# Projections of the differential attention written between the steps of the gated attention's block loop

## The chip, the cores and the metric

The kernel runs on one core of one Trainium2 chip. The metric is the time of one execution on the device in microseconds (us); less is better. Three executions of the kernel before took 1509.5, 1514.04 and 1517.23 us, the median is 1514.04 us. One more execution was recorded by the profiler.

The engines have short names in the profile: PE is TensorE (matrix products), PEld its weight loads, DVE is VectorE, ACT is ScalarE, POOL is GpSimd, SP is the engine whose queue issues most DMA transfers.

## What is computed

Two layers of an encoder on 512 positions of width 1024. Each layer has a mixer and a squared-ReLU MLP, each between norms. The mixer projects the normed input `h` once and splits the result among four head groups; their outputs are joined and projected back.

```
proj = h @ w_in
(a_q, a_k, a_v, a_qi, a_ki, a_wi, b_q, b_k, b_v, b_g,
 c_q, c_k, c_v, c_a, c_g, d_q, d_k, d_v) = jnp.split(proj, ...)
y_a = head_norm(dsa_mixer(a_q, a_k, a_v, a_qi, a_ki, a_wi, pos))     # sparse attention, top-128 selection
y_b = silu(b_g) * head_norm(retention_mixer(b_q, b_k, b_v, pos))
y_c = silu(c_g) * head_norm(gla_mixer(c_q, c_k, c_v, c_a, ...))      # gated linear attention
y_d = head_norm(diff_mixer(d_q, d_k, d_v, pos, ...)) * (1 - lam_init) # differential attention
y = jnp.concatenate([y_a, y_b, y_c, y_d], axis=-1) @ w_out
```

The change touches two of them. The gated linear attention (C) has, within chunks of 64 positions, scores whose decay depends on both positions, and carries a state from chunk to chunk. The differential attention (D) turns its queries and keys by a rotary step (rope), takes two softmax maps per head, subtracts one from the other with a learned factor, and applies the result to its values.

## The kernel before, in words

Everything is in fp32, but the large products are made of three matmuls on split operands: each operand is a high part (a cast on ScalarE) and a low part (the rest, subtracted on VectorE or GpSimd), and `mm3` (line 267) adds high x high, high x low and low x high in PSUM.

`mixers` (line 572) writes the mixer of a layer. The input projection is cut into column groups. A group of 256 columns is projected by `proj_tm` (line 536): for each of four blocks of 128 positions, 24 matmuls (8 slices of the depth, three each) into one of two PSUM buffers of the pool `pj`, and then an eviction that the caller gives. Groups 4, 5 and 6 are the queries, keys and values of D, group 10 the values of C, group 2 the queries of A. The weights of a group come in four tiles, by `prep` (line 254): a DMA of 256 KB on SP's queue into `raw`, the cast to `whi` on ScalarE (line 262), the subtraction to `wlo` on VectorE or GpSimd (line 264). `whi` and `wlo` have a ring of six buffers each, so a group's last tiles can be written only when the group before has been multiplied. `ahead` (line 682) writes the preparation of the next group in a fixed order (10, 4, 5, 6, 2, ...), and `PLAN["lo"]` says on which engine the low parts are made: for group 4 the first on VectorE and three on GpSimd, for group 5 the third on VectorE, for 6 and 2 all on GpSimd. `run` (line 695) is `ahead` and then a projection of all four blocks.

The gated attention is a loop over four blocks `b` (line 901), and in each over four score steps `c` (line 905). `decay` (line 877) makes a block's decay factors: matmuls `fs`, exponentials into `F` on ScalarE, then products into `KF` and `q4` (in the profile `q`) on GpSimd and VectorE; `decay(0)` and the projection of group 10 stand ahead of the loop. A score step copies four pieces of the queries into one of three `QF` tiles on ScalarE (line 913), multiplies them with `KF` into a PSUM tile `sg` (lines 918 and 922; `sg` comes from a pool of three buffers that `fs` and `kv` use too), and VectorE takes the wanted entries of `sg` into `AC` (lines 926 and 928). After the fourth step ScalarE copies `AC` into `AT`, the products `yc` (lines 938 and 940) are made and evicted, and, but for the last block, the state is updated (`tk`, `kt`, `kv`, `S`). `F`, `KF` and `AT` have one buffer each, so blocks follow one another in turn.

The selection of A's keys is made by VectorE in 48 rounds (`top_steps`, line 801, profile lines 809 and 810: a maximum and a replacement); `top(n)` writes some of them at chosen places, here 3 and 2 at the head of the loop's first two blocks and the rest in the later attention blocks.

Behind the loop its memory pool is closed and another one opened, for `QS`, `QD` and `KD`. Then come (line 1098) the projections of groups 4 and 5, the rotary steps of D (`rope`, line 551: four instructions for each block, three blocks on VectorE, one on GpSimd), `d_open(0)` (line 1000: splits and transposes of D's first two blocks into `QD` and `KD`), the projection of group 6, and then the attention blocks of D, A and B with the remaining projections between them, in the order of `PLAN["seq"]`, starting `D00 2.0 D01 2.1`.

All of that is the order in which the program is written. When the program is built, the framework lays out the queue of each engine from it: the written order gives the priority, and an instruction may go ahead of earlier written ones that are not ready by the framework's own reckoning, if buffers are free. On the chip each engine takes its queue in that order.

Of the kernel before, what the change touches and what calls it, by code (L numbers as in the profile page):

```python
# [10 lines left out]
F32 = mybir.dt.float32  # L11
# [10 lines left out]
PLAN = {'ah': {},  # L22
 'ap': 'dddd',
 'ar': 'dddd',
 'blo': 'dppd',
 'br': [0, 0, 0, 1],
 'bst': 2,
 'ce': 's',
 'cp': 1,
 'cq': 'a',  # L30
# [59 lines left out]
P = 128  # L90
# [4 lines left out]
NB = 4  # L95
# [102 lines left out]
def tile_trunk(ctx: ExitStack, tc: tile.TileContext, a, out, dbg=None):  # L198
# [373 lines left out]
    def mixers(l, h, ch):  # L572
# [86 lines left out]
        def tm_tiles(name):  # L659
            return [mx.tile([P, T], F32, name=f"{name}{l}_{b}", tag="tm", bufs=5) for b in range(NB)]  # L660
# [18 lines left out]
        w = {}  # L679
# [15 lines left out]
        def run(g, evict, n=1):  # L695
            ahead(PLAN["ah"].get(str(g), n))
            fill({**PLAN["fA"], **PLAN["fB"]}.get(str(g), 0))
            if isinstance(g, int):
                proj_tm(h, w.pop(g), l, g, evict)
            else:  # L700
                proj_tc(h, w.pop(g), l, g, evict)
# [195 lines left out]
        if PLAN['dc']:  # L897
            ahead_of.append(decay(0))
        run(10, lambda b, ps: center(Vc, b, ps, f"c{l}_{b}"))
        nq = 0  # L900
        for b in range(NB):
            top(PLAN["topc"][b])
# [2 lines left out]
            for c in range(4):  # L905

                Q = QF[nq % 3]
                nq += 1
                for hd in range(4):
                    r = slice(32 * hd, 32 * hd + 32)  # L910
                    e = PLAN["qf"][4 * c + hd]
                    f = {"a": act.copy, "p": pool.tensor_copy, "d": dve.tensor_copy}[e]
                    f(Q[r, :, hd, :], QS4[c // 2][r, 2 * (c % 2):2 * (c % 2) + 2, :])  # L913
                ps = sc.tile([P, 2, 4, 64], F32, name=f"sg{l}_{b}_{c}", tag="sc")
                for i in range(2):
                    lv = 2 * c + i
                    if lv == 7:
                        pe.matmul(ps[0:64, i], KF[:, lv, 0:64], Q[:, i, :, 64:], start=True, stop=True)
                        continue
                    for half in range(2):  # L920
                        t = slice(64 * half, 64 * half + 64)
                        pe.matmul(ps[t, i], KF[:, lv, t], Q[:, i, :, t], start=True, stop=True)  # L922
                for i in range(2):
                    lv = 2 * c + i
                    if lv == 0:
                        dve.tensor_tensor(AL, ps[:, i], eyl.unsqueeze(1).broadcast_to([P, 4, 64]), ALU.mult)
                    elif lv < 7:
                        dve.copy_predicated(AL, lvm[:, lv - 1, :].unsqueeze(1).broadcast_to([P, 4, 64]), ps[:, i])  # L928
                    else:
                        act.copy(AT[0:64, :, 64:], ps[0:64, i])  # L930
# [32 lines left out]
        st1 = ExitStack()  # L963
        s1 = st1.enter_context(tc.tile_pool(name=f"s2{l}", bufs=1, side="right", reuse_waits="tile"))
        QS = s1.tile([P, 4, T], F32R, name=f"QS{l}")
        tmD = tm_tiles("tD")
        Vd = my.tile([P, NB, 256], F32, name=f"Vd{l}")

        def ev_d(g):
            def f(b, ps):  # L970
                act.copy(tmD[b][:, 256 * (g - 4):256 * (g - 4) + 256] if g < 6 else Vd[:, b, :], ps)
            return f

        def ev_a(b, ps):
            tmA = mx.tile([P, T], F32, name=f"tA{l}_{b}", tag="PT", bufs=4)[:, 0:256]
            act.copy(tmA, ps)
# [118 lines left out]
            exp_table(i)  # L1095

        QD, KD, QB, yh = [], [], [], {}
        run(4, ev_d(4))
        run(5, ev_d(5))
        for b in range(NB):  # L1100
            rope(mx, tmD[b].rearrange("p (h d) -> p h d", d=32), "D", b, 16, f"D{l}_{b}", (dve, pool)[PLAN["dr"][b]])
        if PLAN["dp"]:
            d_open(0)
        run(6, ev_d(6))
        opened = []
        for tok in PLAN["seq"].split():
            k = tok[0]
# [291 lines left out]
```

## Time and profile before

| | |
|---|---|
| median of three executions | 1514.04 us (1509.5 to 1517.23) |
| the profiled execution | 1516.26 us, its span 1514.5 us |
| granted TensorE clock over the span | 0.980 |
| gated attention loop, layer 0 | first score matmul at 112.07 us, last `yc` at 167.04 us |
| gated attention loop, layer 1 | first score matmul at 865.25 us, last `yc` at 917.51 us |
| first transposes of `d_open(0)` | 173.87 us and 924.33 us |
| first scores of D (`sd`) | 187.38 us and 937.85 us |

How to read the rows below: a row of the timeline has its start and length in us, the engine, the line of the kernel, the operation and its operands as out<-in, the count, and in brackets the idle time ahead of it with what ended it. A row of waits has the waiting instruction, what it waited for, the total in us, how many times, and the longest. A row by group has the busy total and the mean in ns behind a bar. A row of one tile has the least, median and largest length in ns, and the first and last start. Matmuls are pipelined: their listed length is longer than the distance from one start to the next.

### The profile page before, as it was taken

Reading aid. Unit: us, or ns where it says so; the run is one execution under the profiler, and the core shown is the slowest. Engines: PE = TensorE matmul, PEld = TensorE weight load, DVE = VectorE, ACT = ScalarE, POOL = GpSimd, SP = SyncE. Lnnn points to the kernel's source line nnn. Section 1 sums busy time; section 2 is a strip of 40 time slices with the busy share of each in tenths; the row PEclk is TensorE's granted clock in tenths of the full one; section 3 lists DMA queues with packets and bytes.
Section 4 is the critical chain, followed back from the end, with each engine's and each line's share of the span. In section 5 each row is a group of like instructions: output and inputs, shape, how many; then the busy total and the mean of one; then the engine's idle time right before and its main releaser. Section 6 shows DMA issues by size and latency. Waiting matters only on the chain.

```text
span 1514.5 us, 23722 instructions
## 1 busy us (share of the span) xinstructions
PE 1437.1 (95%) x8578; PEld 1197.6 (79%) x8578; DVE 999.0 (66%) x2203; ACT 745.1 (49%) x1658; POOL 292.4 (19%) x274
## 2 busy tenths in 40 slices
PE   7998989999899979999998999999999999999996
PEld 4685878859798868888997768787798888888896
DVE  8789977776896786434386999764568434343435
ACT  4475677546553322423256765855765433242322
POOL 4333421334200000000032444213430000000001
PEclk8999999989999989999999999999999999999999
DMA  8411222457158886333132112211531433333301
GB/s 326 148 45 29 62 64 85 157 192 251 43 177 283 274 279 196 98 91 98 36 119 79 35 30 78 71 43 43 148 118 44 131 98 97 91 97 96 93 22 56
DMA packets 82269, 171.12 MB, mean 113 GB/s; under 512 B 9284, under 2 KB 16102, under 8 KB 81896
## 3 DMA queue, kind: packets, MB, share of 16 engines
q1 hardware_dynamic: 79524, 167.47, 35.4%
q10 hardware_dynamic: 2628, 2.14, 0.4%
q8 instruction: 67, 1.10, 0.3%
q14 instruction: 50, 0.41, 0.1%
HBM read 165.39 MB, written 4.19 MB: 112 GB/s over the span
## 4 chain that ended last, share of the span: by engine, by line
PE 73%; DVE 18%; ACT 4%; DMA 3%; issue 2%; POOL 1%; SPq 0%; ACTq 0%; DVEq 0%; POOLq 0%
PE pf L269 8%; PE pf L270 8%; PE pf L268 7%; PE p L270 7%; PE p L269 7%; PE p L268 7%; PE ptm L268 3%; PE ptm L269 3%; PE ptm L270 3%; PE first L1184 2%; DMA gw<-modw 2%; DVE ia L810 2%; DVE m L809 2%; PE sb L1077 1%; PE ptc_t L270 1%
## 5 line engine op out<-in xcount | busy, mean ns | idle before, releaser
L262 ACT CAST whi<-raw 128x512 fp32r<-128x512 f32 x388 | 237.6, 621 | 359.6 <-PE p L269 158.2
L264 DVE TENSOR_TENSOR wlo<-raw,whi 128x512 fp32r<-128x512 f32 x266 | 191.0, 723 | 207.5 <-ACT whi L262 204.5
L264 POOL TENSOR_TENSOR wlo<-raw,whi 128x512 fp32r<-128x512 f32 x122 | 166.7, 1386 | 310.9 <-ACT whi L262 268.3
L461 POOL TENSOR_TENSOR sapost<-sapost,sqpost 128x256 f32<-128x256 f32 x16 | 12.3, 770 | 674.1 <-ACT sqpost L459 674.0
L281 DVE CUSTOM_DVE_ANT_0 gw<-gw,cond 128x1024 f32<-128x1024 f32 x80 | 102.1, 1280 | 43.9 <-DMA gw<-modw 43.5
L809 DVE MAX8 m<-ia 128x8 f32<-128x256 f32 (+2 forms) x96 | 53.0, 555 | 1.2
L810 DVE MATCH_REPLACE8 ia<-m,ia 128x256 f32<-128x256 f32 (+2 forms) x96 | 51.9, 541 | 0.1
L913 ACT COPY QF<-q 32x256 f32<-32x256 f32 x120 | 48.4, 403 | 5.2 <-DVE q L890 2.0
L1288 DVE TENSOR_TENSOR rf<-rf,pf 128x512 f32<-128x512 f32 (+1 forms) x80 | 45.7, 573 | 2.4 <-ACT rf L1287 2.4
L1287 ACT ACTIVATE rf<-pf 128x512 f32<-128x512 f32 (+1 forms) x80 | 40.5, 507 | 5.7 <-PE pf L270 5.6
L922 PE MATMUL sg<-QF,KF 128*64 128x256 f32 x224 | 30.4, 395 | 11.0 <-DVE AC L928 8.7
L602 DVE CUSTOM_DVE_ANT_0 sD<-sd,msk 128x128 f32<-128x128 f32 (+3 forms) x64 | 29.7, 487 | 15.8 <-PE sd L1020 9.4
L604 ACT ACTIVATE sD<-sD,mnD 128x128 f32<-128x128 f32 (+3 forms) x64 | 35.5, 559 | 5.2 <-DVE mnD L602 4.8
L1184 PE MATMUL first<-wq,hr 128*128 128x512 f32 x64 | 32.0, 621 | 5.5 <-ACT hr L1205 5.5
L889 POOL TENSOR_TENSOR KF<-F,kc 128x512 f32<-128x512 f32 x16 | 23.7, 1485 | 44.3 <-ACT F L882 43.6
L268 PE MATMUL p<-hd_7h,whi 128*128 128x512 f32 (+1 forms) x80 | 28.6, 358 | 2.7 <-ACT hd_7h L471 2.7
L268 PE MATMUL p<-hd_6h,whi 128*128 128x512 f32 (+1 forms) x80 | 27.9, 349 | 3.4 <-ACT hd_6h L471 3.4
L922 PEld LDWEIGHTS sg<-QF,KF 128*64 128x64 f32 x224 | 14.5, 137 | 20.8 <-issue 14.2
L269 PE MATMUL pf<-h_5l,whi 128*128 128x512 f32 (+1 forms) x80 | 28.0, 350 | 2.8 <-DVE h_5l L515 2.8
L269 PE MATMUL p<-hd_6l,whi 128*128 128x512 f32 (+1 forms) x80 | 28.4, 355 | 0.7 <-DVE hd_6l L472 0.7
L269 PE MATMUL p<-hd_7l,whi 128*128 128x512 f32 (+1 forms) x80 | 28.3, 353 | 0.8 <-DVE hd_7l L472 0.8
L796 DVE SCALAR_TENSOR_TENSOR ia<-rl,wi,ia 128x256 f32<-128x256 f32 (+2 forms) x42 | 27.8, 680 | 1.2
(623 smaller groups left out, 5028.0 us busy)
## 6 DMA issues: line engine op xcount, KB each, us to landing
raw<-w SPq DMA_DIRECT2D x256, 256.0 KB, 2.7
gw<-modw SPq DMA_DIRECT2D x80, 512.0 KB, 4.3
raw<-wtm SPq DMA_DIRECT2D x76, 256.0 KB, 2.8
gs<-modw SPq DMA_DIRECT2D x16, 512.0 KB, 7.1
raw<-wo SPq DMA_DIRECT2D x32, 256.0 KB, 2.8
raw<-wtc SPq DMA_DIRECT2D x24, 256.0 KB, 2.7
xin<-xT SPq DMA_DIRECT2D x8, 256.0 KB, 4.0
wq<-wtm SPq DMA_DIRECT2D x8, 256.0 KB, 6.3
```

The costliest lines, as they stand in the source:

```text
L262: act.copy(hi, raw)
L264: (lo_eng or dve).tensor_tensor(lo, raw, bits(hi), ALU.subtract)
L268: pe.matmul(ps, l[0], r[0], start=start, stop=False)
L269: pe.matmul(ps, l[0], r[1], start=False, stop=False)
L270: pe.matmul(ps, l[1], r[0], start=False, stop=stop)
L281: return dve.tensor_tensor_reduce(raw, raw, cond, 1.0, 0.0, ALU.mult, ALU.add, modT[l][:, c:c + 1])
L809: dve.max(m8, acc)
L810: dve.match_replace(acc, m8, acc, MARK)
L913: f(Q[r, :, hd, :], QS4[c // 2][r, 2 * (c % 2):2 * (c % 2) + 2, :])
L922: pe.matmul(ps[t, i], KF[:, lv, t], Q[:, i, :, t], start=True, stop=True)
L1184: pe.matmul(p, hk, wk, start=k == 0, stop=k == KT - 1)
L1288: dve.tensor_tensor(rl, rl, ps, ALU.mult)
```

## The change

The twelve pieces of the three D projections (group by row block, in the order 4, 5, 6) become `units`. One is written in each score step of the gated loop, behind the score matmuls and ahead of VectorE's reading of them, until they are used up: four in each of the blocks 0, 1 and 2, none in block 3. A unit is the preparation of the next group's weights (at a group's first block), 24 matmuls, the eviction on ScalarE, and for group 5 the rotary step of that row block. `tmD` and `Vd` are allocated ahead of the loop. Behind the loop, `d_open(0)` follows at once, so it now stands behind group 6 and not ahead of it.

```
         run(10, lambda b, ps: center(Vc, b, ps, f"c{l}_{b}"))
+        tmD = tm_tiles("tD")
+        Vd = my.tile([P, NB, 256], F32, name=f"Vd{l}")
+
+        def ev_d(g):
...
+        def unit(g, b):
+            if b == 0:
+                ahead(1)
+            proj_tm(h, w[g], l, g, ev_d(g), [b])
+            if g == 5:
+                rope(mx, tmD[b].rearrange("p (h d) -> p h d", d=32), "D", b, 16, f"D{l}_{b}", (dve, pool)[PLAN["dr"][b]])
+
+        units = [(g, b) for g in (4, 5, 6) for b in range(NB)]
         nq = 0
         for b in range(NB):
             top(PLAN["topc"][b])
...
                     for half in range(2):
                         t = slice(64 * half, 64 * half + 64)
                         pe.matmul(ps[t, i], KF[:, lv, t], Q[:, i, :, t], start=True, stop=True)
+                if units and (b, c) != (NB - 1, 3):
+                    unit(*units.pop(0))
                 for i in range(2):
...
         QD, KD, QB, yh = [], [], [], {}
-        run(4, ev_d(4))
-        run(5, ev_d(5))
-        for b in range(NB):
-            rope(mx, tmD[b].rearrange("p (h d) -> p h d", d=32), "D", b, 16, f"D{l}_{b}", (dve, pool)[PLAN["dr"][b]])
-        if PLAN["dp"]:
-            d_open(0)
-        run(6, ev_d(6))
+        while units:
+            unit(*units.pop(0))
+        d_open(0)
         opened = []
         for tok in PLAN["seq"].split():
```

The definitions of `tmD`, `Vd` and `ev_d` move with it and are otherwise the same. `PLAN["dp"]` is 1, so `d_open(0)` was written before too.

More of the change, by code (lines that the diff above doesn't have):

```diff
@@ L899, in mixers, with f @@
         run(10, lambda b, ps: center(Vc, b, ps, f"c{l}_{b}"))
+        tmD = tm_tiles("tD")
+        Vd = my.tile([P, NB, 256], F32, name=f"Vd{l}")
+        def ev_d(g):
+            def f(b, ps):
+                act.copy(tmD[b][:, 256 * (g - 4):256 * (g - 4) + 256] if g < 6 else Vd[:, b, :], ps)
+            return f
+        def unit(g, b):
[5 more added lines that the diff above has]
+        units = [(g, b) for g in (4, 5, 6) for b in range(NB)]
         nq = 0
@@ L965, in mixers @@
         QS = s1.tile([P, 4, T], F32R, name=f"QS{l}")
[L966 to L972, printed above, removed]
         def ev_a(b, ps):
```

## The prediction

> **What bounds the kernel now.** I read the page first, for the engine that is nearly never free.
>
> ```profile
> span 1514.5 us, 23722 instructions
> ## 1 busy us (share of the span) xinstructions
> PE 1437.1 (95%) x8578; PEld 1197.6 (79%) x8578; DVE 999.0 (66%) x2203; ACT 745.1 (49%) x1658; POOL 292.4 (19%) x274
> ```
>
> TensorE is busy for 95% of the span, so work only changes the time where it fills or opens a hole in TensorE's row. The change moves work inside the gated attention of each layer, so I asked next for TensorE's waits in the two stretches, first 112 to 175 us (layer 0), then 865 to 925 us (layer 1). The columns are total wait, times and longest.
>
> ```profile
> PE sg L922 <- DVE AC L928: 5.2, 1, 5.2
> PE tk L944 <- DVE KF L891: 1.6, 2, 0.9
> ```
> ```profile
> PE sg L922 <- DVE AC L928: 3.5, 1, 3.5
> PE sg L922 <- ACT QF L913: 0.9, 3, 0.3
> PE tk L944 <- DVE KF L891: 0.9, 1, 0.9
> ```
>
> One hole of 5.2 us and one of 3.5 us are most of it: the fourth score product of the first block waits until VectorE has read an earlier score out of PSUM. The table of stretches gives the totals and the clock.
>
> ```profile
> 112.00:175.00 63.00, 55.05 (x408) 42.59 (x407) 59.61 (x153) 39.98 (x101) 27.41 (x29) 0.95 0.12 34
> 865.00:925.00 60.00, 53.72 (x405) 42.04 (x404) 56.44 (x149) 39.59 (x100) 27.14 (x28) 0.97 0.13 36
> 120.00:125.00 5.00, 4.94 (x19) 3.68 (x20) 2.77 (x9) 0.27 (x1) 0.48 (x1) 0.51 0.35 103
> 870.00:880.00 10.00, 8.28 (x51) 7.19 (x52) 8.49 (x27) 3.28 (x9) 5.57 (x6) 0.83 0.36 105
> 177.00:187.00 10.00, 10.00 (x85) 10.00 (x85) 9.65 (x21) 2.72 (x7) 2.01 (x2) 1.00 0.27 73
> 190.00:235.00 45.00, 40.82 (x277) 33.49 (x278) 33.16 (x123) 34.37 (x98) 10.72 (x9) 0.96 0.25 76
> ```
>
> The columns are length, then busy time of TensorE, its weight loads, VectorE, ScalarE and GpSimd, and the granted clock. TensorE is free for 63.00 - 55.05 = 7.95 us in layer 0 and 60.00 - 53.72 = 6.28 us in layer 1, 14.2 us together. Right after the two holes the granted clock is down: 0.51 over 5 us costs 5 x 0.49 = 2.4 us, 0.83 over 10 us costs 1.7 us. So 14.2 + 4.1 = 18.3 us, 1.2% of the span, is all that a better order inside this stage can give. The Trainium skill ("TensorE: Matmul & The Clock Gate", Part 1) says that the clock falls to half after an idle window of about 3.4 us and comes back after about as long of steady work; the two rows agree in depth and in what went before them.
>
> TensorE's timeline around the two holes shows who could have filled them.
>
> ```profile
> 112.07 2.81 PE L922 MATMUL sg<-QF,KF 128*64 128x256 f32 x24
> 120.06 1.12 PE L922 MATMUL sg<-QF,KF 128*64 128x256 f32 x4 [5.18 <-DVE AC L928]
> 120.94 1.06 PE L918 MATMUL sg<-QF,KF 128*64 128x256 f32 x2
> 121.93 0.48 PE L944 MATMUL tk<-ident,KF 128*128 128x128 f32 x1
> 122.06 0.56 PE L268 MATMUL ptm<-whi,h_0h 128*128 128x256 f32 x1
> ...
> 865.25 2.81 PE L922 MATMUL sg<-QF,KF 128*64 128x256 f32 x24
> 871.60 0.65 PE L922 MATMUL sg<-QF,KF 128*64 128x256 f32 x4 [3.54 <-DVE AC L928]
> ```
>
> Two things are to be seen. First, the differential projection (ptm at 122.06) already runs inside the gated loop, although it is written behind it: the build lays it into gaps. So the change is no move from behind the loop into it, but a new order within it. Second, in the first block the build laid no projection between the scores, and TensorE stood.
>
> **The change, part by part.** *Projection units.* Per layer 12 units (groups 4, 5, 6 by four row blocks) of 24 matmuls are now written one behind each score step, so they go to blocks 0 to 2, four each. One matmul costs 10.00 / 85 = 0.118 us (177 to 187 us), a unit 2.8 us, 12 units 34 us. The count is the same as before; only holes matter.
>
> *The first block.* Unit 0 now stands between the first and second score step, which gives VectorE three units, 8.5 us, more until the fourth: both AC waits go, 8.7 us. But unit 0 needs all four weight tiles of group 4, and the low parts of two of them are late. GpSimd's row in layer 0, then the same in layer 1:
>
> ```profile
> L264 POOL TENSOR_TENSOR wlo<-raw,whi x4: 1261/1267/1316, 114.9 to 118.6; 128x512 fp32r<-128x512 f32 x4
> ```
> ```profile
> L264 POOL TENSOR_TENSOR wlo<-raw,whi x4: 1273/1277/1278, 867.7 to 871.4; 128x512 fp32r<-128x512 f32 x4
> ```
>
> By the plan of engines and the ring of six buffers I read the four as tiles 2 and 3 of group 4 and 0 and 1 of group 5. Layer 0: one score step (2.81 / 3 = 0.94) and half a unit (12 x 0.118 = 1.4) end at 112.07 + 2.3 = 114.4; tile 2 is there at 114.9 + 1.27 = 116.2, a wait of 1.8; six matmuls later, at 116.9, tile 3 is due at 117.4, a wait of 0.5. Layer 1: 865.25 + 2.3 = 867.6 against 869.0, then 869.7 against 870.3: 1.4 + 0.6. So 4.3 us of waiting stays, if the second score step stands behind all of unit 0; 0 to 4.3 if the build lets it pass. I take 4.3, the written order. That leaves a gain of 8.7 - 4.3 = 4.4 us. The Trainium skill (same page, Part 2, step 1) states that matmuls stay in program order and only weight loads are pulled ahead: by that rule a stalled unit holds the ready scores behind it and the first block gives the 4.4; if ready matmuls could overtake it would give the 8.7. The 5.18 us in which only a score step was next, with two finished weight tiles at hand, agrees.
>
> *The clock.* Waits of 1.8 us and less: the waits of 0.9 us for KF lie in no stretch of low clock, so I count the 4.1 us as won; 0 to 4.1.
>
> *Blocks 1 and 2.* Of the 14.2 us free time 14.2 - 8.7 = 5.5 us are short waits for KF, QF, AT. With three to four units per block written before the steps that need them, those of blocks 1 and 2 lose their cause; those of block 3 do not.
>
> ```profile
> 149.40 0.70 PE L948 MATMUL kv<-Vc,kt 128*128 128x256 f32 x2
> ...
> 156.13 1.08 PE L922 MATMUL sg<-QF,KF 128*64 128x256 f32 x8 [0.38 <-issue]
> 157.79 1.08 PE L922 MATMUL sg<-QF,KF 128*64 128x256 f32 x8
> 159.16 1.08 PE L922 MATMUL sg<-QF,KF 128*64 128x256 f32 x8 [0.29 <-ACT QF L913]
> 160.78 0.65 PE L922 MATMUL sg<-QF,KF 128*64 128x256 f32 x4
> 161.27 0.59 PE L918 MATMUL sg<-QF,KF 128*64 128x256 f32 x2
> 166.33 0.45 PE L938 MATMUL yc<-AT,Vc 128*64 128x128 f32 x4 [0.20 <-ACT AT L933]
> ```
>
> These are the loop's own matmuls of block 3 in layer 0, with the projections left out by me. Its own short waits are 0.38 + 0.29 + 0.20 = 0.9 us, 1.7 for two layers; of the other 3.8 us I take two thirds, 2.5 us (0 to 3.8).
>
> *Block 3, the price.* Before, projection units filled the time between these rows; now all twelve may be gone. Uncovered, the holes are: from kv's end 150.1 to 156.13, 6.0, less 22 matmuls of the loop that lie there (six of the decay, sixteen of yc), at 0.118 us 2.6, so 3.4; 0.6, 0.3 and 0.5 between score steps; 161.86 to 166.33, 4.5: together 9.3 us per layer. Next in the written order come the first steps of the differential attention and projection 2 (four units, 11.3 us), whose matmuls need nothing that the loop makes. But tiles 2 and 3 of its weights take the buffers of group 6, freed in the middle of the last unit. The casts have their row on the page:
>
> ```profile
> L262 ACT CAST whi<-raw 128x512 fp32r<-128x512 f32 x388 | 237.6, 621 | 359.6 <-PE p L269 158.2
> ```
>
> Two casts of 0.62 and two subtractions of 1.27 us are 3.8 us, against the half unit (1.4) and a score step (0.94) that follow. That is 1.5 us left per layer, 3.0 us; bounds 0 and 9.3 per layer.
>
> *What else is moved.* For each group four weight loads of 256 KB on SP's queue, casts on ScalarE and subtractions on GpSimd (once VectorE), before as after in the order 5, 6, 2; SP has nothing else in the loop, so no queue is passed. Twelve evictions and four rotary steps stand earlier:
>
> ```profile
> L971 ACT COPY tD<-ptm x16: 364/375/380, 135.6 to 924.5; 128x256 f32<-128x256 f32 x16
> ...
> L559 DVE TENSOR_TENSOR r1D<-tD,ccD x6: 284/352/824, 165.0 to 925.5; 128x128 f32<-128x128 f32 x6
> ```
>
> Four evictions of 0.375 per block add 1.5 us to a ScalarE that is busy 39.98 of 63 us: covered. A rotary step begins with 0.35 us and has three shorter ones; VectorE is busy 59.61 of 63 us but mostly with selection rounds that nobody here awaits. Nothing for either. The opening of the differential attention (its transposes) moves behind group 6; the transposes still find TensorE busy, so nothing.
>
> **Sum:** 4.4 + 4.1 + 2.5 - 3.0 = 8.0 us faster. The profiled execution took 1516.26 us (span 1514.5), so it would take 1508.3. Its median sibling is 2.2 us lower, 1514.04 (1509.5 to 1517.23); against that I predict 1506.0.
>
> **The rivals.** *VectorE sets the pace and takes it back.* The first softmax of the differential attention stands behind the last selection round:
>
> ```profile
> 189.65 0.57 DVE L812 TENSOR_SCALAR ia<-ia 128x512 f32<-128x512 f32 x1
> 190.13 0.28 DVE L602 CUSTOM_DVE_ANT_0 sD<-sd,msk 128x128 f32<-128x128 f32 x1
> ```
>
> VectorE is busy 59.61 of 63 us and 9.65 of 10 us before it, so it arrives at 190 whatever TensorE does; TensorE can only run ahead with projection 2, which the next stretch (40.82 of 45 us busy) then lacks. If that stretch keeps its 45 us, the 8 us return as waits there: 1513 (1510 to 1518). Against it: VectorE has 12 us free in that stretch, and later projections can move up.
>
> *Everything goes.* The build lets score steps into the weight waits and projection 2 covers block 3: 8.7 + 4.1 + 3.8 = 16.6, 1497.4.
>
> *Block 3 is bare, slower.* If projection 2 is laid behind the loop, block 3 shows its 9.3 us, and the hole of 4.5 us, as long as those that cost 2.4 and 1.7 us of clock, costs 2.0 more: 11.3 per layer, 22.6, less 4.4 + 4.1 + 2.5 = 11.0: 11.6 slower, 1525.6. It turns slower when more than 5.5 us per layer stay bare, that is with fewer than (11.3 - 5.5) / 2.8 = 2.1 units in block 3. For it: the first block shows that the build leaves holes that it does not foresee. Against it: 122.06 shows it pulling later projections up.
>
> *The order hardly changes,* since the build lays the queues by its own reckoning: 1514.
>
> **How the numbers follow.** Of the last chance 0.05; forecast 0.49, VectorE's pace 0.18, everything 0.14, bare 0.14. The forecast's own range is 1501 to 1511 (4.3 us of weight waits up, some 5 of block 3 down). A measurement of this kernel tells about 0.5% from no change, 7.6 us: faster is below 1506.5, slower above 1521.6. Faster: 0.29 of the forecast, 0.14, and 0.02 of VectorE's: 0.45. Slower: 0.12 of bare and 0.03 for waits that I see no row for: 0.15. Same: 0.40. The range runs from 1495 (past "everything") to 1522; it leaves out most of bare and the ends, under 0.2.
>
> **What would show it.** Right: no AC wait over 2 us in the first block, in its place short waits of ptm for wlo on GpSimd; clock 1.00 there; projection units, the next ones too, between block 3's scores. Wrong: TensorE idle before block 3's scores or before yc for over 3 us (bare); a longer wait of sd for mnD with TensorE earlier there (VectorE's pace); the old pattern of score steps side by side in the first block (same order).

## The result and the profile after

The changed kernel is slower. Its median is 1528.68 us (four executions, 1527.7 to 1534.33) beside 1515.03 us for the kernel before (four, 1509.5 to 1517.23); the ratio is 1.0108 with a 95% interval of 1.0074 to 1.0142, about 14 us. The forecast was 1506.0 us in a range that ended at 1522. The profiled execution took 1528.87 us, and its page begins so:

```profile
span 1527.1 us, 23721 instructions
## 1 busy us (share of the span) xinstructions
PE 1440.8 (94%) x8578; PEld 1199.0 (79%) x8578; DVE 1004.6 (66%) x2203; ACT 744.2 (49%) x1658; POOL 294.1 (19%) x274
```

TensorE has the same 8578 instructions and 3.7 us more busy time, but 12.6 us more span: the time went into holes and into low clock after them. Its longest waits from the gated loop to the first scores of the differential attention, in layer 0 (110 to 196 us) and then in layer 1 (869 to 955 us), in the columns total, times, longest:

```profile
PE sg L938 <- ACT QF L929: 4.0, 3, 2.9
PE yc L956 <- ACT AT L951: 2.6, 2, 2.1
PE ptm L269 <- POOL wlo L264: 1.6, 2, 1.3
```
```profile
PE sg L938 <- ACT QF L929: 4.1, 2, 3.5
PE sg L938 <- issue: 2.0, 2, 1.5
PE yc L956 <- ACT AT L951: 1.4, 2, 0.8
PE ptm L269 <- POOL wlo L264: 1.2, 2, 1.0
```

The two AC waits of 5.2 and 3.5 us are gone, and the forecast's short waits for `wlo` stand in their place. The waits for `QF` and `AT`, 0.3 and 0.2 us in layer 0 before, are now 4.0 and 2.6 us.

To see where the time goes I compared the moments at which both TensorEs had done the same amount of work (each matmul weighted with the median spacing of its kind in the kernel before; one profiled execution of each kernel, times on the kernel before's clock; another weighting moves the figures by up to 0.4 us). In layer 0 the changed kernel goes from 0.9 us ahead at 110 us to 6.7 ahead at 130: the first block's gain. It loses 4.1 us of that between the blocks with indices 0 and 1 (it is 2.6 ahead at 140, and 1.1 of the loss come back by 155) and 4.3 between 1 and 2 (from 3.7 ahead at 155 to 0.6 behind at 165), is 0.7 ahead at 205 and 5.2 behind at 230. In layer 1 it gains 3.1 us in the first block (from 4.4 behind to 1.3), loses 7.1 up to 915 (6.0 of it between 1 and 2), and 2.5 more from 955 to 985.

The place between blocks 1 and 2 of layer 0 shows how. First VectorE's row, then GpSimd's, then TensorE's:

```profile
154.38 1.00 DVE L559 TENSOR_TENSOR r1D<-tD,ccD 128x128 f32<-128x128 f32 x1
155.30 1.30 DVE L560 TENSOR_TENSOR r2D<-tD,ssD 128x64 f32<-128x64 f32 x1
156.52 0.21 DVE L561 TENSOR_TENSOR r2D<-tD,ssD 128x64 f32<-128x64 f32 x1
...
157.32 0.93 DVE L562 TENSOR_TENSOR tD<-r1D,r2D 128x128 f32<-128x128 f32 x1
158.17 0.68 DVE L809 MAX8 m<-ia 128x8 f32<-128x512 f32 x1
158.77 1.14 DVE L975 SCALAR_TENSOR_TENSOR S<-S,F,kv 32x64 f32<-32x64 f32 x4
159.94 0.69 DVE L890 TENSOR_TENSOR q<-F,qc 128x512 f32<-128x512 f32 x1
```
```profile
151.32 5.19 POOL L264 TENSOR_TENSOR wlo<-raw,whi 128x512 fp32r<-128x512 f32 x4 [0.61 <-ACT whi L262]
156.80 1.29 POOL L889 TENSOR_TENSOR KF<-F,kc 128x512 f32<-128x512 f32 x1 [0.29 <-ACT F L882]
160.03 0.31 POOL L968 MEMSET S<- 128x256 f32 x1 [1.93 <-DVE S L975]
160.57 1.38 POOL L889 TENSOR_TENSOR KF<-F,kc 128x512 f32<-128x512 f32 x1 [0.23 <-ACT F L882]
```
```profile
162.49 0.87 PE L938 MATMUL sg<-QF,KF 128*64 128x256 f32 x6 [2.94 <-ACT QF L929]
```

A group has four units and a block takes four, so a group ends with a block. Four low parts on GpSimd (5.19 us; by the ring of six buffers and the plan of engines, the last two of group 6 and the first two of group 2) and a rotary step on VectorE then fall exactly where the next block needs `S`, `KF`, `q` and `QF`. The rotary step stands ahead of `S` in VectorE's queue. Beside GpSimd's subtractions two of its four instructions take 1.30 and 1.00 us, the last takes 0.93 beside `KF`, and the step is done at 158.25. `S` starts at 158.77, the rest of `F` and `KF` wait for it, and TensorE stands for 2.94 us. In layer 1 the rotary step, with one replacement of a round among its four instructions, takes VectorE from 911.24 to 915.96, `S` starts behind it, and TensorE stands for 3.51 us.

Between the blocks 0 and 1 of layer 0 something else happens. The last `sg` of block 0 ends at 126.6 us, but VectorE reads it only at 129.67, behind selection rounds:

```profile
126.32 0.42 DVE L946 COPY_PREDICATED AC<-lvm,sg 128x256 f32<-128x256 uint8 x1
126.71 0.54 DVE L810 MATCH_REPLACE8 ia<-m,ia 128x384 f32<-128x384 f32 x1
...
129.21 0.54 DVE L810 MATCH_REPLACE8 ia<-m,ia 128x384 f32<-128x384 f32 x1
129.67 0.43 DVE L946 COPY_PREDICATED AC<-lvm,sg 128x256 f32<-128x256 uint8 x1
```

`AT` follows that read, `yc` waits 2.1 us for `AT`, and the clock from 131 to 140 us is 0.81, which costs 1.7 us: 3.8 of the 4.1 us lost there.

In the differential stage (first `sd` to the first head norm) the second loss shows, first in the kernel before, then after (length; busy time and records of TensorE; its weight loads, VectorE, ScalarE, GpSimd; granted clock):

```profile
187.40:231.40 44.00, 37.94 (x260) 31.11 (x259) 32.78 (x117) 31.87 (x92) 13.32 (x12) 0.96 0.28 84
```
```profile
196.00:236.70 40.70, 33.18 (x208) 26.53 (x207) 28.74 (x105) 30.18 (x86) 9.48 (x8) 0.87 0.21 65
```

52 matmuls, 6.1 us at 0.118, are done earlier now, but the stage is only 3.3 us shorter: fewer projections are left to fill its holes, and the clock falls to 0.87.

### The profile page after: what moved, and what is told of

Same layout as the page of the kernel before. It is cut to its first block, busy times and chain, and to the rows that moved or that the text cites. A ratio compares the mean times of both kernels' runs of the same rounds, so it can differ in the third digit from the quotient of the medians.

```text
span 1527.1 us, 23721 instructions
## 1 busy us (share of the span) xinstructions
PE 1440.8 (94%) x8578; PEld 1199.0 (79%) x8578; DVE 1004.6 (66%) x2203; ACT 744.2 (49%) x1658; POOL 294.1 (19%) x274
## 4 chain that ended last, share of the span: by engine, by line
PE 66%; DVE 19%; DMA 6%; ACT 4%; issue 3%; POOL 1%; SPq 0%; ACTq 0%; DVEq 0%; POOLq 0%
PE pf L269 6%; PE p L268 6%; PE p L269 6%; PE p L270 6%; PE pf L270 6%; PE pf L268 6%; DMA gw<-modw 5%; PE ptm L268 3%; PE ptm L270 2%; PE ptm L269 2%; DVE ia L810 2%; PE first L1190 2%; DVE m L809 2%; PE ptc_t L268 1%; PE ptc_t L270 1%
## 5 line engine op out<-in xcount | busy, mean ns | idle before, releaser
L938 PE MATMUL sg<-QF,KF 128*64 128x256 f32 x224 | 33.9, 420 | 10.8 <-ACT QF L929 8.1
L268 PE MATMUL ptm<-whi,h_0h 128*128 128x256 f32 x76 | 27.9, 367 | 2.0 <-ACT tI L742 1.1
```

What stands on the lines that cost most here:

```text
L268: pe.matmul(ps, l[0], r[0], start=start, stop=False)
```

## The experiments

Three theories stood at the start. **Theory 1:** the first block's gain is real and is handed back where a group's weight preparation and the rotary steps land, ahead of what the next block or the differential stage waits for. **Theory 2:** it is handed back because group 6 and `d_open` come in another order, so the differential stage lacks filler. **Theory 3:** in the expectations of e1 to e4, units written ahead of scores hold back the gated chain by TensorE's order alone; from e9 on, VectorE's queue is full of selection rounds, and every reordering is late by them. All ratios are to the kernel before on the same chip, with 95% intervals. The last column is the time from the first `sg` to the first head norm matmul `hs`, both layers added, in the profiled execution; it holds the loop and the first part of the differential stage.

| kernel | median us | ratio | sg to hs, us |
|---|---|---|---|
| before | 1512.1 to 1515.0 (by job) | 1 | 231.9 |
| after | 1528.7 | 1.0108 (1.0074 to 1.0142) | 244.6 |
| e1 rotary steps written behind | 1529.7 | 1.0089 (1.0057 to 1.0121) | 246.0 |
| e2 group 6 behind the loop | 1517.0 | 1.0016 (0.9997 to 1.0035) | 235.9 |
| e3 three units a block | 1518.7 | 1.0017 (0.9995 to 1.0039) | 236.7 |
| e4 units in the first block only | 1524.7 | 1.0066 (1.0045 to 1.0087) | 239.4 |
| e5 low parts on VectorE | 1524.9 | 1.0079 (1.0048 to 1.0111) | 243.4 |
| e6 rotary steps held | 1517.5 | 1.0036 (1.0015 to 1.0057) | 237.6 |
| e7 = e2 + held | 1515.9 | 1.0016 (0.9994 to 1.0039) | 232.7 |
| e8 group 6 in the last block | 1519.9 | 1.0039 (1.0019 to 1.0059) | 237.7 |
| e9 after, no rounds | 1513.2 | 1.0007 (0.9992 to 1.0023) | 229.3 |
| e10 before, no rounds | 1499.1 | 0.9908 (0.9883 to 0.9934) | 215.0 |
| e11 = e7 + low parts on VectorE | 1517.0 | 1.0035 (1.0016 to 1.0053) | 235.2 |
| e12 before + low parts on VectorE | 1519.9 | 1.0044 (1.0017 to 1.0072) | 242.5 |
| e13 before, early rounds held | 1517.8 | 1.0017 (1.0003 to 1.0031) | 236.9 |
| e14 after, no low parts | 1515.0 | 1.0005 (0.9989 to 1.0021) | 233.4 |
| e15 before, no low parts | 1511.0 | 0.9972 (0.9957 to 0.9987) | 230.3 |
| **e16 before, early and late rounds held** | **1505.4** | **0.9947 (0.9925 to 0.9970)** | **223.6** |
| e17 before, late rounds held | 1514.4 | 1.0008 (0.9985 to 1.0031) | 234.6 |
| e18 = e7 + late rounds held | 1520.0 | 1.0048 (1.0028 to 1.0068) | 240.0 |

### e1: the rotary steps written behind the loop

```
             proj_tm(h, w[g], l, g, ev_d(g), [b])
-            if g == 5:
-                rope(mx, tmD[b]..., "D", b, 16, ...)
...
         while units:
             unit(*units.pop(0))
+        for b in range(NB):
+            rope(mx, tmD[b]..., "D", b, 16, ...)
         d_open(0)
```

> All twelve units stay in the loop; only the rotary steps of D are written behind the loop again. Theory 1 (each group of four units ends with a block, so the weight preparation of the next group, its low parts on GpSimd, and the rotary steps land where the next block's decay products, state and query copies are wanted): the rotary steps are one of the two things that land between the blocks with indices 1 and 2, where the trace after lost about 3 to 4 us in each layer; without them 2 us a layer come back, 1524 to 1526, and the pieces of QF are no longer late there. Theory 2 (the loss is d_open and the late projections missing in the differential stage): no change, 1528. Theory 3 (units written ahead hold back the gated chain by TensorE's order alone): no change, 1528.

Measured 1.0089, level with after. The row of VectorE says why nothing was learnt of the theories: the build laid the steps where they had been, within 0.5 us.

```profile
154.84 1.00 DVE L559 TENSOR_TENSOR r1D<-tD,ccD 128x128 f32<-128x128 f32 x1
155.76 1.30 DVE L560 TENSOR_TENSOR r2D<-tD,ssD 128x64 f32<-128x64 f32 x1
...
159.23 1.13 DVE L973 SCALAR_TENSOR_TENSOR S<-S,F,kv 32x64 f32<-32x64 f32 x4
```

The written place only sets a priority; to move an instruction it must be ordered behind another one (e6).

### e2: group 6 behind the loop

```
-        units = [(g, b) for g in (4, 5, 6) for b in range(NB)]
+        units = [(g, b) for g in (4, 5) for b in range(NB)]
...
-        while units:
-            unit(*units.pop(0))
         d_open(0)
+        for b in range(NB):
+            unit(6, b)
```

> Only groups 4 and 5 are units of the loop; d_open and then group 6 stand behind it, as in the kernel before. Theory 2: the 5.2 and 2.6 us that the trace after lost in the differential stages come back, 1520 to 1521. Theory 1: the losses between the blocks stay, 7 us in each layer, since the preparation of group 6 still falls between indices 1 and 2; of the differential stage's loss at most half comes back: 1524 to 1528. Theory 3: a third of the units is out of the way, but only those of the block with index 2, where little was lost: 1526.

Measured 1.0016: more comes back than theory 2 asked for, theory 1 expected 1524 or more. In layer 0 the lag stays the same as in after until 165 us, and the differential stage then ends 2.1 us ahead of the kernel before, not 5.2 behind. In layer 1 some 7 us are lost between blocks, as in after. Theory 3 as it stood here (1526) does not fit.

### e3: three units in each block

```
-                if units and (b, c) != (NB - 1, 3):
+                if units and c < 3:
```

> Three units in each of the four blocks, none behind a fourth score step, so a group of four no longer ends with a block and block 3 has three units of its own. Theory 1: the preparation of a group moves into the middle of a block, half or more of the 14 us lost between blocks comes back: 1517 to 1521. Theory 2: the last units come later still, so the differential stage has no more work than before: 1527 to 1530. Theory 3: as many units are written ahead of scores as before, 1526 to 1529.

Measured 1.0017, in theory 1's range; but three units in block 3 also leave more projection for the end, as in e2, so this run alone does not tell the two apart. It speaks against theory 3 as it stood here (1526 to 1529).

### e4: units in the first block only

```
-        units = [(g, b) for g in (4, 5, 6) for b in range(NB)]
+        units = [(g, b) for g in (4,) for b in range(NB)]
...
+        for b in range(NB):
+            unit(5, b)
+        for b in range(NB):
+            rope(mx, tmD[b]..., "D", b, 16, ...)
         d_open(0)
+        for b in range(NB):
+            unit(6, b)
```

> Only the four units of group 4 stand in the loop, in the first block; groups 5 and 6, the rotary steps and d_open stand behind it as in the kernel before. All three theories keep the gain of the first block (6 us in layer 0, 3 us in layer 1 by the lag of equal TensorE work). Theory 1: the change from the first to the second block still has the preparation of group 5 and loses 3 us a layer, the second to third loses nothing: 1509 to 1512. Theory 2 and 3: nothing is lost later, 1505 to 1507. If it stays above 1516, the gain of the first block is no gain at all, and all of it is handed back by what VectorE owes later.

Measured 1.0066: a miss for all three theories; it falls under the expectation's last sentence. The first block gains 4.2 us in layer 0 and 3.0 in layer 1, and both are gone by the end of the loop. What moved is not only what was written earlier: with group 4 done, the build pulls group 5, its preparation and its rotary steps into the next blocks. In layer 1 the first product of a rotary step took 1.37 us beside a subtraction on GpSimd, between block 3's AC reads, and `yc` waited 2.8 us for `AT`. From the first `sg` to the first `hs`, layer 0 is level with the kernel before (119.2 us against 119.3) and layer 1 is 7.8 us longer; the rest of that I did not trace.

### e6: the rotary steps held in VectorE's queue

`after(x, y)` orders `y` behind `x` on one engine and adds no wait; `i` holds the first three products of `rope`.

```
-            dve.tensor_tensor(QI, F[:, 8, :], qs, ALU.mult)
+            qi[b] = dve.tensor_tensor(QI, F[:, 8, :], qs, ALU.mult)
...
+        for n in i:
+            if kind == "D" and e is dve:
+                after(qi[2], n)
```

> The kernel after with D's rotary steps written behind the loop, and those on VectorE held, in its queue, behind the product qi of the block with index 2. (Writing them behind alone left them where they were: the rows of that run show r1D at 154.84 us, ahead of S, as in the kernel after.) Theory 1, now narrowed to VectorE's queue: rotary step, S and q of the next block stand in one queue, so the steps delay S, S delays the last part of F, and QF comes late; with the steps behind, the holes of 3.2 us (layer 0) and 3.8 us (layer 1) before the third block's first scores shrink to about 1 us each: 5 us less than after, 1523 to 1525. Theory 2 (the differential stage lacks filler): no part of it is touched, 1527 to 1530.

Measured 1.0036: 11 us come back by the ratios, 7 by the last column, more than the 5 that theory 1 expected. VectorE's row at the same place, and TensorE's:

```profile
155.96 1.14 DVE L978 SCALAR_TENSOR_TENSOR S<-S,F,kv 32x64 f32<-32x64 f32 x4
157.13 1.77 DVE L895 TENSOR_TENSOR q<-F,qc 128x512 f32<-128x512 f32 x1
...
161.58 0.42 DVE L562 TENSOR_TENSOR r2D<-tD,ssD 128x64 f32<-128x64 f32 x1
```
```profile
160.76 1.08 PE L941 MATMUL sg<-QF,KF 128*64 128x256 f32 x8 [1.35 <-ACT QF L932]
```

`S` starts 2.8 us earlier and the hole shrinks from 2.94 to 1.35 us; `q` now runs beside GpSimd and takes 1.77 us where it took 0.69. The rest of the gain is in the differential stage of layer 0, where this run lost nothing (after: 5.9 us) although its matmuls there stand almost in the order of after; in layer 1 it lost 4.0 us there (after: 2.5).

### e7: e2 and e6 together

> Groups 4 and 5 in the loop, rotary steps held behind the third block's products, then d_open and group 6 behind the loop. If the two causes add: 1517.0 (group 6 behind) less the 4 to 5 us of the two holes, 1511 to 1514, which would be level with the kernel before or 2 us below it. If the hole before the third block has another cause (GpSimd's low parts ahead of the products KF, casts ahead of QF on ScalarE): 1516 to 1518.

Measured 1.0016, the same as e2 alone within the intervals: the two do not add, or by less than the intervals show. GpSimd's four subtractions (5.00 us from 152.03) still stand ahead of its `KF`, VectorE's `q` and `KF` take 1.76 and 1.34 us beside GpSimd, and TensorE stands 1.9 us there for VectorE's `KF`.

### e8: group 6 in the last block

```
-                if units and (b, c) != (NB - 1, 3):
+                if units and b != 2:
```

> The kernel after with the four units of group 6 in the last block in place of the third; d_open still behind group 6. Theory 2a (what counts is how much projection work is left for the last block and the differential stage): as with group 6 behind the loop, 1516 to 1519. Theory 2b (what counts is that d_open is written ahead of group 6): as after, 1527 to 1530.

Measured 1.0039, 1519.85 us: just above 2a's range, far from 2b's. `d_open` is still written behind group 6, so most of the difference comes from where the units of group 6 stand (and with them the preparation of the next group), not from the place of `d_open`. The 0.2% to e2 may be its share; the intervals do not tell.

### e5: the low parts of groups 5, 6 and 2 on VectorE

```
- 'lo': {'4': 'dppp', '5': 'ppdp', 't4': 'dddd'},
+ 'lo': {'4': 'dppp', '5': 'dddd', '6': 'dddd', '2': 'dddd', 't4': 'dddd'},
```

> The kernel after with all low parts of groups 5, 6 and 2 made on VectorE, so GpSimd has none of them and is free for KF, q and the state's memset. If the rotary steps and the products between the blocks are slow because both engines work at once (a rotary product took 1.30 us beside a subtraction on GpSimd, 0.21 us without), the holes between blocks and those of 2.0 and 2.8 us in the differential stage of layer 0 shrink: 1519 to 1524. If it is VectorE's queue that counts, its extra subtractions make it later: 1529 to 1535.

Measured 1.0079, hardly better than after. The place between blocks 1 and 2 heals as theory 1 said (2.0 us ahead of the kernel before at 165, 2.4 at 915, where after is 0.6 and 8.4 behind), and the differential stage takes it back: 4.5 us in layer 0 from 200 to 230, some 9 in layer 1 from 950 to 975. Four subtractions that this run leaves on GpSimd (of the groups behind 2, 203.35 to 209.32 us) lie there, and VectorE's steps beside them took 1.26, 1.26, 1.50 and 1.62 us, as in after (see e14).

### e11 and e12: held steps with low parts on VectorE, and its control

e11 is e7 with `'5': 'dddd', '6': 'dddd'`; e12 is the kernel before with the same.

> Group 6 behind the loop, rotary steps held, and the low parts of groups 5 and 6 made on VectorE in place of GpSimd (group 2's stay on GpSimd). In the run without the last part GpSimd's four subtractions (5.00 us from 152.03) still stood ahead of the products KF and q of the third block, and VectorE's q, KF and qi took 1.76, 1.34 and 1.37 us beside GpSimd's work: the third block's scores waited 2.2 us at 158. If that is what is left, 2 us in each layer come back: 0.3% below that run, 0.997 to 1.000 of the kernel before. If VectorE's eight more subtractions (0.6 to 0.7 us each, in a queue with little room) cost as much: 1.001 to 1.004.

> The kernel before with the same low parts on VectorE and nothing else: the control for the run beside it. In the kernel before the AC wait of the first block and the holes of the differential stage have VectorE as the releaser, so nothing is gained: 0.999 to 1.004 of the kernel before. If it is faster by as much as the run beside it, the place of the projections has no part in that gain.

Measured 1.0035 and 1.0044. In the kernel before, the subtractions cost 0.4% more on VectorE than on GpSimd, and e11 is no faster than e7: this is no way out.

### e9 and e10: without the selection rounds

```
-                    m8 = mx.tile([P, 8], F32, ...)
-                    dve.max(m8, acc)
-                    dve.match_replace(acc, m8, acc, MARK)
                     yield
```

> The kernel after without the 48 selection rounds of each layer (the maxima and replacements are left out, so the sparse attention sees a mask without a selection). Theory 3 (VectorE's in-order queue, full of rounds, is what hands the gain back): with the queue free, after is 6 us or more faster than before without rounds. Theories 1 and 2 (GpSimd's subtractions and the place of the projections): the holes between blocks and in the differential stage stay, after without rounds is 3 to 13 us slower than before without rounds.

> The kernel before without the 48 selection rounds of each layer, to be compared with the run beside it. If the 5.2 us and 3.5 us AC waits of the first block are made by rounds in VectorE's queue they go, and this kernel is 10 us or more below the kernel before; if the build's order alone makes them (only a score step is next while VectorE reads the earlier ones), they stay.

The kernel before gains 0.9%, the changed one ends 14.1 us above it, as much as with the rounds: the rounds alone do not make the loss. They have a part in it all the same. Without them the first block has nothing to win (e9 is 1 us ahead of e10 at 130 us, where with the rounds the changed kernel is 6.7 ahead), and the loss between the blocks 0 and 1 of layer 0 is below 1 us in place of 4.1. So the rounds made both the gain and a part of the loss, and the equal distance hides it. In e10 the first block has no AC wait at all; its waits from 105 to 170 us are

```profile
PE sg L919 <- ACT QF L910: 1.1, 4, 0.3
PE tk L941 <- DVE KF L888: 0.4, 1, 0.4
PE ptm L268 <- ACT Vc L855: 0.3, 1, 0.3
```

So the hole that the change filled was made by the rounds. In the kernel before, the first score step ended by 113.0 and its AC read stood behind five microseconds of VectorE's work, most of it rounds:

```profile
113.73 0.42 DVE L809 MAX8 m<-ia 128x8 f32<-128x256 f32 x1
...
115.96 0.54 DVE L810 MATCH_REPLACE8 ia<-m,ia 128x384 f32<-128x384 f32 x1
116.42 1.15 DVE L812 TENSOR_SCALAR ia<-ia 128x256 f32<-128x256 f32 x1
...
118.62 0.41 DVE L926 TENSOR_TENSOR AC<-sg,eyl 128x256 f32<-128x256 f32 x1
```

### e14 and e15: without GpSimd's subtractions

```
+        if skip:
+            return hi, hi
         lo = pl.tile(shape, F32R, ...)
         (lo_eng or dve).tensor_tensor(lo, raw, bits(hi), ALU.subtract)
```

`skip` is set for groups 5, 6, 2 and t2.

> The kernel after without the low parts of the weight groups 5, 6, 2 and t2: their high part is multiplied in place of the low one, so TensorE's work is the same and the 16 subtractions of each layer (15 on GpSimd, one on VectorE) are left out. To be compared with the run beside it. If GpSimd's subtractions at the block boundaries and in the differential stage (VectorE's products took 1.26 to 1.62 us there beside them, 0.22 to 0.62 without) make the give-back, after is now 5 to 12 us below before with the same left out. If the place of the projections makes it (no projection left for the differential stage), after stays 5 us or more above.

> The kernel before without the same low parts. In the kernel before GpSimd's subtractions lie mostly where VectorE makes selection rounds that nobody awaits, so little is gained: 2 to 6 us below the kernel before.

The loss shrinks from 14 us to 4.0 (1515.01 less 1511.0): neither end was right. Some 10 us of the loss need the subtractions; the other 4 do not. Between the blocks 1 and 2, e14 loses some 1.5 us in each layer (after: 4.3 and 6.0); between 0 and 1 of layer 0 it loses 3.8, as after does. The differential stage of after shows how the subtractions act there, VectorE's row and GpSimd's:

```profile
204.24 1.36 DVE L562 TENSOR_TENSOR tA<-r1A,r2A 128x64 f32<-128x64 f32 x1
...
205.71 1.26 DVE L1038 TENSOR_SCALAR sD<-sD,rcD,nlam 128x384 f32<-128x384 f32 x1
...
207.56 1.49 DVE L652 TENSOR_TENSOR hlDk<-tD,hlDk 128x256 fp32r<-128x256 f32 x1
208.98 1.62 DVE L1039 SCALAR_TENSOR_TENSOR sD<-sD,rcD,sD 128x384 f32<-128x384 f32 x1
```
```profile
204.22 2.53 POOL L264 TENSOR_TENSOR wlo<-raw,whi 128x512 fp32r<-128x512 f32 x2 [7.12 <-ACT whi L262]
207.33 2.85 POOL L264 TENSOR_TENSOR wlo<-raw,whi 128x512 fp32r<-128x512 f32 x2 [0.57 <-ACT whi L262]
```

The same four steps took 0.22, 0.48, 0.41 and 0.62 us in e6, where they did not meet a subtraction (one other split did, 1.49 us): 4.0 us more in VectorE's queue, which TensorE with few projections left waits out. Such steps alone do not make the loss. In e8 four steps of this stage are as slow (1.54, 1.24, 1.35 and 1.30 us from 205 to 215), and layer 0 loses nothing there; e2 has the same. So a shift of a few microseconds can decide what this stage costs, as in e6's layer 0, unless projections are left to cover it, as in layer 0 of e2 and e8.

### e13: the kernel before, its early rounds held

`acr[0]` is the last AC read on VectorE in the first block.

```
-                    dve.max(m8, acc)
+                    n = dve.max(m8, acc)
+                    if 16 * (b - 1) + r >= 12:
+                        after(acr[0], n)
```

> The kernel before, projections where they were, with the selection rounds from the thirteenth on held, in VectorE's queue, behind the last AC read of the first block. Without rounds the kernel before had no AC wait in the first block and was 0.9% faster, so the rounds in the queue make that wait. If it can be had by order alone, the 8.7 us of waits and 4.1 us of low clock go, and VectorE ends its rounds some 3 us later in each layer, of which the differential stage has 12 us to spare: 0.992 to 0.996 of the kernel before. If VectorE's pace decides, all is handed back at the first scores of the differential attention: 0.998 to 1.002.

Measured 1.0017. Both AC waits are gone, and TensorE is 7 us ahead of the kernel before until 185 us in layer 0. Its longest wait from 170 to 240 us, and VectorE's row at its end:

```profile
PE sd L1026 <- DVE mnD L604: 4.3, 1, 4.3
```
```profile
184.95 0.69 DVE L811 MAX8 m<-ia 128x8 f32<-128x512 f32 x1
185.56 0.27 DVE L604 CUSTOM_DVE_ANT_0 sD<-sd,msk 128x128 f32<-128x128 f32 x1
```

`sd` was there at 180.3, the softmax stands behind the rounds until 185.56. Layer 1 waits in the same way: the first scores are there at 923.5, the softmax starts at 928.8. This is the prediction's rival "VectorE sets the pace", in a kernel that moves no projection.

### e16, e17 and e18: the late rounds held too

To e13 (e16), to the kernel before (e17) and to e7 (e18) this adds, for the last eight of the 48 rounds, an order behind `dsm`, the last softmax minimum of D00, D01, D02 and D03 in turn:

```
+                    k = 16 * (b - 1) + r
+                    if k >= 40:
+                        after(dsm[(k - 40) // 2], n)
```

> The kernel before, projections where they were, with two groups of selection rounds moved back in VectorE's queue: from the thirteenth on behind the first block's last AC read, and the last eight in pairs behind the last softmax scores of the first four blocks of the differential attention. With the first hold alone TensorE was 7 us ahead in layer 0 at 190 us and then waited 4.3 us for mnD, because the softmax stood behind the last rounds. If VectorE's rounds are what hands the gain back, some 5 us in each layer stay: 0.992 to 0.996 of the kernel before. If the differential stage has no room for eight rounds (1.4 us each, 11.4 us; VectorE was free for 12 us there): 0.999 to 1.004.

> The kernel before with only the last eight rounds moved into the differential stage. The first block's waits (8.7 us and 4.1 us of clock) stay, the wait of sd for mnD (2.4 us in layer 0) goes: 0.997 to 1.000. If VectorE's rounds in the differential stage delay its chain: 1.001 to 1.005.

> Groups 4 and 5 in the loop with the rotary steps held and group 6 behind (1.0016 of the kernel before), and the last eight rounds moved into the differential stage. If the first block's gain of the moved projections is real and only VectorE's rounds hand the rest of it back: 0.994 to 0.998. If the holes at the block boundaries and GpSimd's subtractions hold it: no change, 1.000 to 1.003.

e16 measured 0.9947 (0.9925 to 0.9970), 1505.4 us: faster than both kernels, with the projections where they were. Its profiled span is 1501.5 us, and the same wait is

```profile
PE sd L1033 <- DVE mnD L606: 1.8, 3, 0.7
```

From the first `sg` to the first `hs` the granted clock is 1.00 in both layers (before 0.96 and 0.98, after 0.93 and 0.97). Neither half does it alone (1.0017 and 1.0008). The gain is uneven: of the 8.3 us in the last column 7.3 lie in layer 0; layer 1 gives most of its first block's gain back, its differential stage takes 43.5 us where the kernel before takes 39.9. e18, with moved projections and the same late hold, is at 1.0048, above e7. It loses in the stage that the eight rounds were moved into: 43.4 and 44.3 us there against 39.4 and 39.2 in e7, with VectorE busy for 40.4 of the 43.4 us against 30.3 of 39.4. So with the projections moved, this hold costs more than it frees; which of its steps TensorE waits for I did not trace.

## Why the prediction was wrong

*The first block (4.4 us of waits, 4.1 of clock): right.* The AC waits of 8.7 us went, 2.8 us of waits for `wlo` came (forecast 4.3), and the lead grew by 5.8 and 3.1 us, 8.9 together against 8.5. The stalled unit did hold the ready scores behind it: the second score step begins at 117.4 us, behind the whole of unit 0.

*The clock: right where it was read, wrong as a gain.* The first block ran at full clock, but each new hole of 2 us and more brought a new stretch of low clock: four rows, the first block, the places between blocks 0 and 1 and between 1 and 2, and the differential stage, all of layer 0 after:

```profile
111.00:125.00 14.00, 12.40 (x96) 10.00 (x95) 13.62 (x41) 3.48 (x9) 6.69 (x7) 1.00 0.25 77
131.00:140.00 9.00, 7.75 (x50) 7.01 (x50) 8.60 (x17) 6.46 (x18) 8.28 (x7) 0.81 0.42 117
160.00:170.00 10.00, 7.51 (x46) 5.12 (x46) 8.85 (x19) 7.28 (x18) 3.36 (x4) 0.83 0.00 0
205.00:235.00 30.00, 22.48 (x121) 16.80 (x121) 18.98 (x62) 20.34 (x55) 7.15 (x6) 0.83 0.28 88
```

*Blocks 1 and 2 (2.5 us won): the step that failed.* "Those of blocks 1 and 2 lose their cause": they gained one, and some 7 us were lost there in each layer. The error lies in "What else is moved ... Nothing for either". I counted the rotary steps by their own length and asked whether VectorE was awaited, not what stands behind them in its queue: `S`, and through it `F`, `KF`, `q` and `QF`. And I looked for weight preparation that changes its order against other preparation ("no queue is passed"), not for what it would run beside. The last rotary step on VectorE, priced at 0.35 us and three shorter ones, took 3.4 us in layer 0 (1.00, 1.30, 0.21 and 0.93) and 4.3 in layer 1 (1.37, 1.30, 1.33 and 0.28), because it met GpSimd's work. The row that I had shown for it had a longest time of 824 ns, and the kernel before has the same meeting, where nobody waited for it:

```profile
175.70 1.30 DVE L560 TENSOR_TENSOR r2D<-tD,ssD 128x64 f32<-128x64 f32 x1
```
```profile
173.10 5.07 POOL L264 TENSOR_TENSOR wlo<-raw,whi 128x512 fp32r<-128x512 f32 x4
```

The runs separate the two. At the same place in layer 0, the four instructions of that step take 0.28, 0.22, 0.22 and 0.27 us in e14, without the subtractions, and `S` starts at 154.62 us in place of 158.77. Of the 4.3 and 6.0 us lost between the blocks 1 and 2, some 2.5 stay in each layer with the rotary steps held (e6), some 1.5 without the subtractions (e14); without the rounds 4.7 and 3.0 stay (e9). GpSimd's own `KF` came late by them only in layer 1, where it starts directly behind them (913.72); in layer 0 it waited for `F`. The loss between the blocks 0 and 1 of layer 0 has another cause, which the prediction's "mostly with selection rounds that nobody here awaits" passed over: nobody awaits the rounds, but the last AC read stood behind them. It stays at 4.0 us in e6 and 3.8 in e14 and is below 1 us without the rounds (e9).

*Block 3 (3.0 us lost, 0 to 9.3): covered, and paid later.* Its largest gap is 0.77 us in layer 0 and 0.58 in layer 1, since projection 2 was pulled up as forecast. I let that cover be free; the same 52 matmuls were then missing in the differential stage, where 5.9 us were lost in layer 0 and 2.5 in layer 1. That `d_open` costs nothing where it stands held as far as e8 shows: 0.2% to e2 at most. The rival "VectorE sets the pace" came nearest ("TensorE can only run ahead with projection 2, which the next stretch then lacks"), but named the wrong waiter: `sd` waits no more for `mnD`; `thA` and `tpD` wait for splits and casts.

*The rival that ended slower* (block 3 bare, 1525.6) gave nearly the right time by luck: the holes that it names did not occur.

*What the whole reading missed:* the AC wait was taken for a lack of filler on TensorE. It was VectorE's queue, with work ahead that nobody awaited, and the row of VectorE from 113 to 119 us would have shown it.

What stays open: how the loss of some 4 us without the subtractions divides beyond the 3.8 us between the blocks 0 and 1 of layer 0; why the same changes act so differently in the differential stages of the two layers; and which steps make e18 slower than e7.

## What to carry to other kernels

When an engine waits, read the row of the engine it waits for, and ask what that engine did in the meantime: if it is work that nobody awaits, move that work back, and do the same at the next place where the lead would be lost, or the gain is only carried there. When work is moved into a loop, its side work goes along: list on every queue which step of the loop now stands behind it and what it will run beside on the other engines, price it by its longest time in the trace and not by its usual one, and look where a weight group ends within the loop. Filler that is used early is missing later; a hole is only closed when the later one has been looked at too.

## What the hardware showed that I had not expected

VectorE's instructions with two operands in SBUF do not slow down a little beside GpSimd, they wait: a product of 128x64 took 0.21 us alone and 1.30 us beside subtractions of 1.3 us each, `q` 0.69 and 1.77 us beside GpSimd's `KF` of 1.31, while the rounds' replacements stayed at 0.67 us and the AC reads out of PSUM at 0.43. A step with one tile and two columns of scalars (`sD`, line 1038) was slowed as well, from 0.48 to 1.26 us. The Trainium skill ("SBUF — State Buffer", section "Who interferes with whom") states that a VectorE instruction with two SBUF inputs contends with a GpSimd instruction that reads SBUF, and that the port pair they share is an exclusive lock; the rows of the two-operand steps agree. So in this kernel such a step, when it meets a run of subtractions, is better priced with GpSimd's duration than with its own.
